# Twelve mixing matmuls in a row, and other places for the side work of an output projection

## The chip, the cores and the metric

The kernel runs on one core of a Trainium2 chip. The metric is the time of one execution on the device in microseconds; lower is better.

## The reference

One layer of a chunked gMLP block with a widened inner dimension, then a last RMSNorm. With DEPTH = 1 only mixer A runs. All values are float32; x is (1, 1024, 2048), the inner width E is 4096.

```python
CHUNK, A_GROUPS = 128, 8

def rmsnorm(x, g):
    y = x * lax.rsqrt(jnp.mean(x * x, axis=-1, keepdims=True) + EPS)
    return y * g

def gmlp_mixer(h, w_in, v_gain, w_s, b_s):
    z = h @ w_in                                    # (1024, 2048) @ (2048, 3 * 4096)
    u, v, gate = jnp.split(z, 3, axis=-1)
    u = gelu(u)
    v = rmsnorm(gelu(v), v_gain)
    vc = v.reshape(bsz, seq // CHUNK, CHUNK, A_GROUPS, A_GROUP_DIM)
    sv = einsum('gpq,bnqgc->bnpgc', w_s, vc) + b_s.T[None, None, :, :, None]
    return u * sv.reshape(bsz, seq, D_INNER), gate

h = rmsnorm(x, a_norm)
y, gate = gmlp_mixer(h, a_w_in, a_v_gain, a_w_s, a_b_s)
x = x + (y * silu(gate)) @ a_w_out                  # (1024, 4096) @ (4096, 2048)
out = rmsnorm(x, final_norm)
```

## The kernel before, in words

**Products.** Both projections are done by a seven-product scheme on 2 x 2 blocks (Strassen's): each operand of a product is a block or the sum or difference of two blocks (A_OF, B_OF), and a product goes into one or two blocks of the result. Each operand is split into a high and a low part (split, L84: ScalarE makes hi, VectorE makes lo), and each matmul is three (mm3, L89: hi*hi at L91, hi*lo at L92, lo*hi at L93). A step is one k-range of 256 rows: 2 x 4 x 3 = 24 matmuls of 128 x 512.

**Input projection.** 12 strips of columns: first four strips with v, then eight strips, one for each group g, with u and gate. In a strip seven products (IN_ORDER) of four steps each. Feeding runs two steps ahead (feed(i + AHEAD): w_sum and w_lo on VectorE, w_hi on ScalarE, into six "hl" slots, so three steps' pairs), loads three steps ahead (LOADS, on SP's queue).

**Mixing.** Of group g it runs beside products in two halves of four chunks each (apply_spatial): the first half in product 6 of its own strip (k = 6), the second half in product 1 of the next strip (k = 10); that of the last group in the first product of the output projection. A half uses four PSUM banks: two tiles of two banks each (bank_set), chunk m in bank m % 2 of tile m // 2. A chunk takes three matmuls (sv) and one VectorE instruction that reads them (L312, with the bias and u * silu(gate)). The two pairs of PSUM tiles alternate between the products and the mixing, so the product that starts two steps after a second half uses its banks next.

**Side work.** Results of the mixing are transposed in 32 x 32 blocks on VectorE (finish_y, four transposes an item, 16 items a half) and stored to DRAM through POOL's queue (L345); the output projection loads them back from there (load_y, L141, POOL's queue). Such items wait in a list `later` with a cost each; after the matmuls of each step `work(us)` takes items until their costs reach its argument (2.8 by default). Items in `soon` (readers of finished products) are all taken, and their costs count too.

**Output projection.** Seven products (OUT_ORDER = 3, 5, 2, 4, 1, 7, 6), each for two column halves s of eight steps. In s = 0 the a operand is fed (a_sum, a_hi, a_lo: two more VectorE operations), and s = 1 uses the same tiles; they take 16 slots of tag "ax" for a product, except steps 5 to 7 of the first product, which take "big" slots. The residual x is loaded into 16 "big" tiles o (L456), the products are added to them (L462), and their squares are summed on ScalarE (squares, L469).

**Last norm.** The gain of the norm is loaded into two "ax" tiles fn_b (L509) and multiplied in by items times_fn (L476). finish_rows(h, m) sums the squares of 128 rows (L482), takes the root (L81 on VectorE, L82 on POOL), scales four blocks (L490 on VectorE, L492 on ScalarE) and stores them (L494, SP's queue). The first half of the rows (h = 0) is finished from `later` during the last product; the second half behind the last matmuls, which are ordered row block by row block (L532).

**Order.** The program is written in this order; a scheduler then places each instruction on its engine's queue by that order and by what it depends on, and puts in the waits. Each engine and each DMA queue works off its own queue in order.

Of the kernel before, what the change touches and what calls it, by code (L numbers as in the profile page):

```python
# [10 lines left out]
ALU = mybir.AluOpType  # L11
# [8 lines left out]
A_OF = {1: (11, 1, 22), 2: (21, 1, 22), 3: (11,), 4: (22,), 5: (11, 1, 12), 6: (21, -1, 11), 7: (12, -1, 22)}  # L20
B_OF = {1: (11, 1, 22), 2: (11,), 3: (12, -1, 22), 4: (21, -1, 11), 5: (22,), 6: (11, 1, 12), 7: (21, 1, 22)}
IN_ORDER = (1, 2, 5, 4, 3, 7, 6)
OUT_ORDER = (3, 5, 2, 4, 1, 7, 6)
# [7 lines left out]
def gmlp_kernel(ctx, tc, x, xT, g_in, w_in, gain, wsT, bsT, w_out, fnorm, out):  # L31
    nc = tc.nc
# [3 lines left out]
    HCH = NCH // 2  # L36
    HT = S // 2
    G = wsT.shape[0]
    C = E // G
    CB = C // P  # L40
    JI = D // P // 4
    JO = E // P // 4
# [9 lines left out]
    def slot(tag, name, dt=F32):  # L52
        return main.tile([P, 2, C], dt, tag=tag, name=name, bufs=SLOTS[tag])

    def bank_set(n, name):

        return [ps.tile([P, 2, 512], F32, tag=f"set{n}_{t}", name=f"{name}_{t}") for t in range(2)]
# [20 lines left out]
    def inv_rms(ss, width, r):  # L78

        m = m_all if ss.shape[1] > 1 else main.tile([P, 1], F32, tag="m_inv", name="m_inv", bufs=2)  # L80
        nc.vector.tensor_scalar(out=m, in0=ss, scalar1=1.0 / width, scalar2=EPS, op0=ALU.mult, op1=ALU.add)  # L81
        nc.gpsimd.tensor_tensor(out=r, in0=m, in1=mhalf[:, : ss.shape[1]], op=ALU.pow)  # L82
# [6 lines left out]
    def mm3(acc, ah, al, bh, bl, start, stop, on=False):  # L89

        nc.tensor.matmul(out=acc, lhsT=ah, rhs=bh, start=start, stop=False, skip_group_check=on)  # L91
        nc.tensor.matmul(out=acc, lhsT=ah, rhs=bl, start=False, stop=False, skip_group_check=on)  # L92
        nc.tensor.matmul(out=acc, lhsT=al, rhs=bh, start=False, stop=stop, skip_group_check=on)  # L93

    def combine(of, load, tag, name):

        if len(of) == 1:
            return load(of[0])
        a, b = load(of[0]), load(of[2])
        s = slot("sum", name)  # L100
        nc.vector.tensor_tensor(out=s, in0=a, in1=b, op=ALU.add if of[1] > 0 else ALU.subtract)  # L101
        return s
# [4 lines left out]
    outs = [(0, C), (2 * C, 3 * C)]  # L107
# [83 lines left out]
    def feed(i):  # L191

        if i >= len(steps):
            return
        kind, s, p, j = step = steps[i]
        first = kind == "in" and s == 0
        if first or (kind == "out" and s == 0):
            load = h_block if first else load_y
            raw = combine(A_OF[p], lambda b: load(step, b), "sum", "a_sum")

            tag = "big" if kind == "out" and p == OUT_ORDER[0] and j >= JO - 3 else "ax"
            parts = [slot(tag, f"a_{l}", F32R) for l in ("hi", "lo")]
            split(raw, *parts)
            aparts[i] = parts
            if first:
                for t, d in zip(parts, a_dram[p, j]):
                    nc.gpsimd.dma_start(out=d, in_=t.bitcast(F32))
        elif kind == "out":
            aparts[i] = aparts[i - JO]
        raw = combine(B_OF[p], lambda b: load_w(step, b), "sum", "w_sum")  # L210
        wparts[i] = [slot("hl", f"w_{l}", F32R) for l in ("hi", "lo")]
        split(raw, *wparts[i])


    soon, later = [], []

    def work(us=2.8):
        while soon or (later and us > 0):
            cost, what = (soon or later).pop(0)
            us -= cost  # L220
            what()

    def work_all():
# [7 lines left out]
        out=eye, in_=ones[:, 0, :P], pattern=[[-1, P]], compare_op=ALU.is_equal, fill=0.0, base=0, channel_multiplier=1)  # L231
    ss_x, r_ps = bank_set(1, "ss_x")
    order_x = [(jj, h) for j in range(JI) for jj in (j, JI + j) for h in range(2)]
    for n, (jj, h) in enumerate(order_x):
        t = hx[jj, h] = slot("big", "x_t")
        nc.sync.dma_start(
            out=t, in_=xT[jj * 2 * P:(jj + 1) * 2 * P, h * HT:(h + 1) * HT].rearrange("(u p) c -> p u c", p=P))
# [16 lines left out]
    for h in range(2):  # L254
        for n in range(HCH):
            nc.vector.tensor_scalar(
                out=d_x[:, h, n * P:(n + 1) * P], in0=eye, scalar1=rx[:, h * HCH + n:h * HCH + n + 1], scalar2=None,
# [47 lines left out]
    def apply_spatial(g, half, n_set, prod):  # L305
        banks = bank_set(n_set, f"sv{g}_{half}")
        for m in range(HCH):
            sv = banks[m // 2][:, m % 2]
            wh, wl, vh, vl = spatial[half * HCH + m]
            mm3(sv, wh, wl, vh, vl, True, True)  # L310
            y = prod[m // 2][:, m % 2]
            nc.vector.scalar_tensor_tensor(  # L312
                out=y, in0=sv, scalar=bs_sb[:, g:g + 1], in1=y, op0=ALU.add, op1=ALU.mult)
        for m in range(HCH):
            for part in range(P // Q):
                later.append((1.2, lambda m=m, part=part: finish_y(g, half, m, part, prod[m // 2])))
# [55 lines left out]
    for s in range(len(strips)):  # L372
# [5 lines left out]
        if is_v:  # L378
            gains = slot("ax", "gain_b")
            nc.gpsimd.dma_start(  # L380
                out=gains.rearrange("p a b -> p (a b)"),
# [64 lines left out]
    fn_b = []  # L446
# [25 lines left out]
    def times_fn(s, block, t, cs=(0, 1)):  # L472
        n = outs[s][block % 10 - 1] // C
        for c in cs:
            d = acc[s, block][t][:, c]
            nc.vector.tensor_tensor(out=d, in0=d, in1=fn_b[n // 2][:, n % 2], op=ALU.mult)  # L476

    def finish_rows(h, m):

        ss = main.tile([P, 1], F32, tag="ss", name="ss", bufs=4)  # L480
        ro = main.tile([P, 1], F32, tag="ro", name="ro", bufs=4)
        nc.vector.tensor_reduce(out=ss, in_=sso[h][:, m], axis=mybir.AxisListType.X, op=ALU.add)  # L482
        inv_rms(ss, D, ro)
        r0 = (h * HCH + m) * P
        for s in range(2):
            for n in range(2):
                block = 10 * (h + 1) + n + 1
                d = acc[s, block][m // 2][:, m % 2]
                if n == 0:
                    nc.vector.tensor_scalar(out=d, in0=d, scalar1=ro, scalar2=None, op0=ALU.mult)  # L490
                else:
                    nc.scalar.activation(out=d, in_=d, func=AF.Copy, scale=ro)  # L492
                col = outs[s][n]
                nc.sync.dma_start(out=out[r0:r0 + P, col:col + C], in_=d)  # L494

    n_set = a
    for p in OUT_ORDER:
        for s in range(len(outs)):
            n_set ^= 1
            banks = bank_set(n_set, f"o{p}_{s}")  # L500
            last = p == OUT_ORDER[-1] and s == 1
            for j in range(JO):
                if j == JO // 2:
                    for block, _ in TO_C[p]:
                        init_acc(s, block)
                    if p == OUT_ORDER[-1] and s == 0:
                        for n in range(2):
                            fn_b.append(slot("ax", f"fn_b{n}"))
                            nc.gpsimd.dma_start(  # L509
                                out=fn_b[n].rearrange("p a b -> p (a b)"),  # L510
                                in_=fnorm[:, 2 * n * C:2 * (n + 1) * C].broadcast_to([P, 2 * C]))
                        for s_, block in finished:
                            for t in range(2):
                                later.append((1.4, lambda s_=s_, block=block, t=t: times_fn(s_, block, t)))
                        for m in range(HCH):
                            later.append((1.2, lambda m=m: finish_rows(0, m)))
                if p == OUT_ORDER[0] and s == 0 and j < 3:
                    spatial_step(8 + j, *before)
                advance(i)
                if not last or j < JO - 2:  # L520
                    products(i, banks, True)
                work()
                i += 1
            if last:

                work_all()
                for m in range(HCH):
                    for ii in (i - 2, i - 1):
                        products(ii, banks, True, (m,))
                    block = DONE_AFTER[p][0]  # L530
                    d = acc[s, block][m // 2][:, m % 2]
                    nc.vector.tensor_tensor(out=d, in0=d, in1=banks[m // 2][:, m % 2], op=ALU.add)  # L532
                    squares(s, block, m // 2, (m % 2,))
                    times_fn(s, block, m // 2, (m % 2,))
                    finish_rows(1, m)
                continue
            for t in range(2):
                soon.append((1.2 * len(TO_C[p]), lambda p=p, s=s, t=t, banks=banks: add_to(s, p, t, banks)))
            for block in DONE_AFTER[p]:
                finished.append((s, block))  # L540
                for t in range(2):
                    soon.append((0, lambda s=s, block=block, t=t: squares(s, block, t)))
                    if p == OUT_ORDER[-1]:
                        later.append((1.4, lambda s=s, block=block, t=t: times_fn(s, block, t)))


# [32 lines left out]
```

## Time and profile before

| | |
|---|---|
| median of 3 runs | 2641.49 us (2640.5 to 2643.14) |
| the profiled execution | 2639.87 us |
| its span in the profile | 2638.2 us |
| TensorE, matmuls | 2538.4 us busy, 96% of the span, 10980 matmuls |
| VectorE | 1801.9 us busy, 68% |
| ScalarE | 856.6 us busy, 32% |
| mean granted TensorE clock | 0.982 |
| DMA | 701.92 MB, mean 266 GB/s |

The rows of the timeline are: start, duration, engine, line, operation, output<-inputs, sizes, count; in brackets the idle time of the engine before the instruction and what released it. A name such as w_lo stands for all buffers of that name. A row of waits reads: who waited, for whom, us in total, times, longest. Matmuls overlap: one lasts 0.39 us in the rows, but the next starts 0.23 us after it.

### The profile page before, as it was taken

What the parts mean: (1) busy time and instruction counts of PE and PEld (TensorE: products, weight loads), DVE (VectorE), ACT (ScalarE), POOL (GpSimd) and SP (SyncE); (2) the same over time, 40 slices, a digit from 0 to 9 for tenths busy, and PEclk for the clock granted to TensorE, in tenths of its full rate; (3) what the DMA queues carried; (4) which work ended last, traced back from release to release, by engine and by line L of the source; (5) the groups of instructions that cost most, each with busy time, mean ns of one, the idle gap of its engine ahead of it and who ended that gap; (6) DMA issues with size and microseconds to landing.
All of it is one profiled execution on the core that took longest, in us unless ns stands there. A gap on an engine that the chain in (4) does not pass through costs nothing.

```text
span 2638.2 us, 29702 instructions
## 1 busy us (share of the span) xinstructions
PE 2538.4 (96%) x10980; PEld 2076.4 (79%) x10980; DVE 1801.9 (68%) x2466; ACT 856.6 (32%) x1008; POOL 163.7 (6%) x289
## 2 busy tenths in 40 slices
PE   6999999999999999999999999999999999999997
PEld 3887888888887887878878788787887788888876
DVE  6984545546458768587685876858769946577776
ACT  4452332323233232322423224233243223233233
POOL 1220000000000000000000000000010211011010
PEclk8999999999999999999999999999999999999999
DMA  8998786959685785856858568586695856669884
GB/s 311 352 414 310 290 294 225 362 200 362 236 303 189 238 315 190 316 196 245 316 180 314 212 239 327 173 297 239 215 355 179 302 200 222 225 228 320 288 296 167
DMA packets 250049, 701.92 MB, mean 266 GB/s; under 512 B 21665, under 2 KB 21681, under 8 KB 249905
## 3 DMA queue, kind: packets, MB, share of 16 engines
q1 hardware_dynamic: 210816, 557.91, 59.3%
q0 software_dynamic: 39088, 142.11, 14.2%
q8 instruction: 87, 1.43, 0.2%
q14 instruction: 58, 0.47, 0.1%
HBM read 628.63 MB, written 71.30 MB: 265 GB/s over the span
## 4 chain that ended last, share of the span: by engine, by line
PE 79%; DVE 11%; issue 5%; DMA 4%; POOL 0%; ACT 0%; SPq 0%; POOLq 0%; ACTq 0%; DVEq 0%
PE m L93 21%; PE m L92 20%; PE m L91 20%; PE o L93 6%; PE o L92 6%; PE o L91 6%; DVE y_t L341 4%; DVE w_lo L87 2%; DMA w_raw<-in_w_in 2%; DMA x_t<-in_xT 1%; DVE c L312 1%; DVE w_sum L101 1%; DMA y_raw<-y 1%; DVE u L418 1%; DVE o L476 1%
## 5 line engine op out<-in xcount | busy, mean ns | idle before, releaser
L92 PE MATMUL m<-w_lo,a_hi 128*128 128x512 f32 x2688 | 1050.8, 391 | 7.1 <-DVE w_lo L87 7.1
L91 PE MATMUL m<-w_hi,a_hi 128*128 128x512 f32 x2688 | 1052.1, 392 | 3.8 <-ACT a_hi L86 3.5
L93 PE MATMUL m<-w_hi,a_lo 128*128 128x512 f32 x2688 | 1052.3, 391 | 0.0
L87 DVE TENSOR_TENSOR w_lo<-w_sum,w_hi 128x1024 fp32r<-128x1024 f32 x320 | 391.2, 1223 | 387.6 <-ACT w_hi L86 386.7
L86 ACT ACTIVATE w_hi<-w_sum 128x1024 fp32r<-128x1024 f32 x320 | 339.3, 1060 | 950.7 <-PE m L92 623.2
L92 PEld LDWEIGHTS m<-w_lo,a_hi 128*128 128x128 f32 x2688 | 507.9, 189 | 115.0 <-DVE w_lo L87 8.8
L91 PEld LDWEIGHTS m<-w_hi,a_hi 128*128 128x128 f32 x2688 | 508.2, 189 | 112.7 <-ACT a_hi L86 5.0
L93 PEld LDWEIGHTS m<-w_hi,a_lo 128*128 128x128 f32 x2688 | 508.3, 189 | 106.8 <-DVE a_lo L87 0.6
L101 DVE TENSOR_TENSOR w_sum<-w_raw 128x1024 f32<-128x1024 f32 x319 | 388.3, 1223 | 113.6 <-DMA w_raw<-in_w_in 101.2
L92 PE MATMUL o<-w_lo,a_hi 128*128 128x512 f32 x896 | 350.8, 391 | 9.7 <-DVE w_lo L87 9.7
L93 PE MATMUL o<-w_hi,a_lo 128*128 128x512 f32 x896 | 349.9, 391 | 2.2 <-DVE a_lo L87 2.2
L91 PE MATMUL o<-w_hi,a_hi 128*128 128x512 f32 x896 | 350.1, 391 | 1.6 <-DVE m_inv L81 1.4
L341 DVE STREAM_TRANSPOSE y_t<-c 32x128 f32<-32x128 f32 x1024 | 309.8, 303 | 15.6
L86 ACT ACTIVATE w_hi<-w_raw 128x1024 fp32r<-128x1024 f32 x128 | 135.5, 1060 | 510.4 <-PE m L92 360.3
L87 DVE TENSOR_TENSOR w_lo<-w_raw,w_hi 128x1024 fp32r<-128x1024 f32 x128 | 156.6, 1223 | 173.5 <-ACT w_hi L86 172.9
L92 PEld LDWEIGHTS o<-w_lo,a_hi 128*128 128x128 f32 x896 | 169.0, 189 | 47.9 <-DVE w_lo L87 12.8
L91 PEld LDWEIGHTS o<-w_hi,a_hi 128*128 128x128 f32 x896 | 169.0, 189 | 37.9 <-DVE m_inv L81 1.8
L93 PEld LDWEIGHTS o<-w_hi,a_lo 128*128 128x128 f32 x896 | 168.9, 189 | 38.0 <-DVE a_lo L87 3.1
L86 ACT ACTIVATE a_hi<-a_sum 128x1024 fp32r<-128x1024 f32 (+1 forms) x61 | 63.4, 1044 | 132.2 <-DVE a_sum L101 122.4
L141 POOL DMA_DIRECT2D y_raw<-y x96 | 50.9, 531 | 495.7 <-DVE w_sum L101 206.4
L87 DVE TENSOR_TENSOR a_lo<-a_sum,a_hi 128x1024 fp32r<-128x1024 f32 (+1 forms) x61 | 73.2, 1203 | 11.3 <-ACT a_hi L86 11.3
L91 PE MATMUL sv<-v_hi,ws_hl 128*128 128x512 f32 x64 | 29.6, 463 | 47.2 <-DVE c L312 47.2
(88 smaller groups left out, 1119.0 us busy)
## 6 DMA issues: line engine op xcount, KB each, us to landing
w_raw<-in_w_in SPq DMA_DIRECT2D x224, 512.0 KB, 6.8
w_raw<-in_w_out SPq DMA_DIRECT2D x192, 512.0 KB, 6.7
y_raw<-y POOLq DMA_DIRECT2D x96, 512.0 KB, 6.6
a_hi<-a_0h SPq DMA_DIRECT2D x77, 512.0 KB, 5.3
a_lo<-a_0l SPq DMA_DIRECT2D x77, 512.0 KB, 5.2
a_hi<-a_1h SPq DMA_DIRECT2D x77, 512.0 KB, 6.0
a_lo<-a_1l SPq DMA_DIRECT2D x77, 512.0 KB, 4.9
a_hi<-a_2h SPq DMA_DIRECT2D x77, 512.0 KB, 5.8
```

Of the source, the lines that this page charges most:

```text
L86: nc.scalar.activation(out=hi, in_=raw, func=AF.Copy)
L87: nc.vector.tensor_tensor(out=lo, in0=raw, in1=hi.bitcast(F32), op=ALU.subtract)
L91: nc.tensor.matmul(out=acc, lhsT=ah, rhs=bh, start=start, stop=False, skip_group_check=on)
L92: nc.tensor.matmul(out=acc, lhsT=ah, rhs=bl, start=False, stop=False, skip_group_check=on)
L93: nc.tensor.matmul(out=acc, lhsT=al, rhs=bh, start=False, stop=stop, skip_group_check=on)
L101: nc.vector.tensor_tensor(out=s, in0=a, in1=b, op=ALU.add if of[1] > 0 else ALU.subtract)
L141: nc.gpsimd.dma_start(out=yraw[key], in_=y_dram[g][block // 10 - 1][:, b:b + 2, :])
L312: nc.vector.scalar_tensor_tensor(out=y, in0=sv, scalar=bs_sb[:, g:g + 1], in1=y, op0=ALU.add, op1=ALU.mult)
L341: nc.vector.transpose(out=yt[q * Q:(q + 1) * Q, :, c * P + i * Q:c * P + (i + 1) * Q], in_=yv[i * Q:(i + 1) * Q, :, q, :])
L418: nc.vector.tensor_tensor(out=cs[block][t], in0=cs[22][t], in1=banks[t], op=ALU.add)
L476: nc.vector.tensor_tensor(out=d, in0=d, in1=fn_b[n // 2][:, n % 2], op=ALU.mult)
```

## The change

In apply_spatial the loop over the four chunks is split in two: first all twelve matmuls, then the four readers. The rest touches the output projection: which slots some a operands take, how much side work a step takes, when fn_b is loaded, when the first half of the rows is finished, which engine scales which block, and, in the last rows, a tile of its own for the product with the gain.

```diff
@@ feed
-            tag = "big" if kind == "out" and p == OUT_ORDER[0] and j >= JO - 3 else "ax"
+            out_j = j if kind == "out" else -1
+            tag = "big" if (p == OUT_ORDER[0] and out_j >= JO - 4) or (p == OUT_ORDER[-1] and out_j == JO - 1) else "ax"
@@ apply_spatial
             wh, wl, vh, vl = spatial[half * HCH + m]
             mm3(sv, wh, wl, vh, vl, True, True)
+        for m in range(HCH):
+            sv = banks[m // 2][:, m % 2]
             y = prod[m // 2][:, m % 2]
             nc.vector.scalar_tensor_tensor(
                 out=y, in0=sv, scalar=bs_sb[:, g:g + 1], in1=y, op0=ALU.add, op1=ALU.mult)
@@ finish_rows
-    def finish_rows(h, m):
+    ros, last_block = {}, {}
+
+    def scale_rows(h, m):
         ss = main.tile([P, 1], F32, tag="ss", name="ss", bufs=4)
         ro = main.tile([P, 1], F32, tag="ro", name="ro", bufs=4)
         nc.vector.tensor_reduce(out=ss, in_=sso[h][:, m], axis=mybir.AxisListType.X, op=ALU.add)
         inv_rms(ss, D, ro)
+        ros[h, m] = ro
+
+    def finish_rows(h, m):
+        ro = ros.pop((h, m))
         r0 = (h * HCH + m) * P
         for s in range(2):
             for n in range(2):
                 block = 10 * (h + 1) + n + 1
                 d = acc[s, block][m // 2][:, m % 2]
-                if n == 0:
+                if (s, block) == (1, 22):
+                    d = last_block[m]
+                if n == s:
                     nc.vector.tensor_scalar(out=d, in0=d, scalar1=ro, scalar2=None, op0=ALU.mult)
                 else:
                     nc.scalar.activation(out=d, in_=d, func=AF.Copy, scale=ro)
@@ loop of the output projection
-                    if p == OUT_ORDER[-1] and s == 0:
+                    if p == OUT_ORDER[-2] and s == 1:
                         for n in range(2):
                             fn_b.append(slot("ax", f"fn_b{n}"))
...
                                 later.append((1.4, lambda s_=s_, block=block, t=t: times_fn(s_, block, t)))
+                    if p == OUT_ORDER[-1] and s == 1:
                         for m in range(HCH):
-                            later.append((1.2, lambda m=m: finish_rows(0, m)))
+                            later.append((0.3, lambda m=m: scale_rows(0, m)))
+                        for m in range(HCH):
+                            later.append((0.9, lambda m=m: finish_rows(0, m)))
...
-                work()
+                work(2.8 if s == 1 else 0.6 if len(A_OF[p]) > 1 else 1.6)
@@ last rows
                     squares(s, block, m // 2, (m % 2,))
-                    times_fn(s, block, m // 2, (m % 2,))
+                    if m % 2 == 0:
+                        scaled = slot("hl", "o_fn")
+                    n = outs[s][block % 10 - 1] // C
+                    nc.vector.tensor_tensor(out=scaled[:, m % 2], in0=d, in1=fn_b[n // 2][:, n % 2], op=ALU.mult)
+                    last_block[m] = scaled[:, m % 2]
+                    scale_rows(1, m)
                     finish_rows(1, m)
@@ behind a product
-                    if p == OUT_ORDER[-1]:
+                    if fn_b:
                         later.append((1.4, lambda s=s, block=block, t=t: times_fn(s, block, t)))
```

## The prediction

> **What bounds the kernel now.** I read the page first, then the waits of TensorE, then busy time by stretches, then the timeline of the stretches where time is lost. The page's line of engines:
>
> ```profile
> PE 2538.4 (96%) x10980; PEld 2076.4 (79%) x10980; DVE 1801.9 (68%) x2466; ACT 856.6 (32%) x1008; POOL 163.7 (6%) x289
> ```
>
> TensorE is the bound, VectorE is second. The waits of TensorE (total us, times, longest):
>
> ```profile
> PE sv L91 <- DVE c L312: 47.2, 8, 6.4
> PE o L92 <- DVE w_lo L87: 9.7, 7, 2.8
> PE o L93 <- DVE a_lo L87: 2.2, 2, 1.4
> PE o L91 <- DVE m_inv L81: 1.4, 1, 1.4
> ```
>
> The largest is the wait the diff aims at: mixing matmuls (sv) wait for the VectorE reader of other mixing results, eight times, once a half. The others belong to the output projection. Stretches (length, busy time and count of each engine, granted clock, DMA):
>
> ```profile
> core 0: us, PE busy (x) PEld busy (x) DVE busy (x) ACT busy (x) POOL busy (x), PEclk, DMA share, GB/s
> 841.00:842.00 1.00, 1.00 (x4) 0.71 (x4) 0.39 (x2) 0.00 (x0) 0.00 (x0) 0.50 0.00 0
> 846.00:848.00 2.00, 2.00 (x10) 1.64 (x9) 1.70 (x5) 0.00 (x0) 0.00 (x0) 1.00 0.00 0
> 1984.00:2030.00 46.00, 42.57 (x180) 34.38 (x179) 44.84 (x89) 16.75 (x16) 1.26 (x2) 0.96 0.48 156
> 2030.00:2100.00 70.00, 62.79 (x269) 49.54 (x268) 63.14 (x102) 17.70 (x17) 14.94 (x25) 1.00 0.76 265
> 2100.00:2500.00 400.00, 400.00 (x1767) 331.31 (x1766) 257.32 (x221) 125.73 (x149) 35.64 (x65) 1.00 0.72 249
> 2560.00:2610.00 50.00, 45.95 (x194) 37.10 (x193) 42.93 (x62) 18.14 (x26) 2.23 (x4) 0.97 0.61 209
> 2600.00:2605.00 5.00, 5.00 (x24) 4.14 (x23) 3.18 (x4) 1.06 (x1) 0.00 (x0) 1.00 0.00 0
> 2610.00:2638.00 28.00, 15.46 (x67) 11.90 (x65) 10.26 (x25) 8.23 (x16) 2.16 (x4) 0.87 0.41 150
> ```
>
> The undisturbed stretch 2100 to 2500 gives the pace: 400 us / 1767 = 0.2264 us a matmul. Time lost in a stretch is its length less its count times that: 1984 to 2100 loses 116 - 449 x 0.2264 = 14.4 us, 2560 to 2610 loses 6.1, 2610 to 2638 loses 12.8 (most of it the unavoidable end).
>
> **Part 1, the mixing (L305 to L313), seven times in the input projection.** Timeline of one second half:
>
> ```profile
> 832.42 0.39 PE L91 MATMUL sv<-v_hi,ws_hl 128*128 128x512 f32 x1
> 832.62 6.64 DVE L341 STREAM_TRANSPOSE y_t<-c 32x128 f32<-32x128 f32 x21
> 839.30 0.75 DVE L312 SCALAR_TENSOR_TENSOR c<-sv,bs_sb,c 128x512 f32<-128x512 f32 x1
> 840.10 0.79 PE L91 MATMUL sv<-v_hi,ws_hl 128*128 128x512 f32 x1 [6.38 <-DVE c L312]
> 1007.22 0.79 PE L91 MATMUL sv<-v_hi,ws_hl 128*128 128x512 f32 x1 [6.38 <-DVE c L312]
> ```
>
> Two groups of three run (the second starts at 832.42); a third starts only when the reader L312 of 839.30 is done. That reader reads another bank of the same two-bank PSUM tile, so the wait goes by whole tiles. On VectorE it stands behind 21 transposes (6.64 us, 0.316 each). From the clock column: after this idle stretch TensorE runs at 0.50 at 841 and is at 1.00 only by 846. The price of one stall comes from the period: 1007.22 - 840.10 = 167.12 us for 28 steps of 24 matmuls and 24 mixing ones, 696 x 0.2264 = 157.6, lost 9.5 us: some 6.5 of idling and 3 of half clock.
>
> The edit puts all twelve matmuls ahead of the four readers in program order. No matmul then depends on a reader of its own half. The cost: the reader of m=0 now waits for the group of m=1, same tile, at least one group of 3 x 0.23 = 0.7 us later; hidden, as VectorE is busy with the 21 transposes until 839.3 anyway. Nothing is added to or taken from any engine. So 7 x 9.5 = 66.5 us would go, if nothing else is late.
>
> What is late next is VectorE. Today the stall lets it catch up:
>
> ```profile
> 841.79 1.41 DVE L312 SCALAR_TENSOR_TENSOR c<-sv,bs_sb,c 128x512 f32<-128x512 f32 x2 [0.61 <-PE sv L93]
> 846.23 0.75 DVE L312 SCALAR_TENSOR_TENSOR c<-sv,bs_sb,c 128x512 f32<-128x512 f32 x1 [1.44 <-PE sv L93]
> 850.28 1.23 DVE L87 TENSOR_TENSOR w_lo<-w_raw,w_hi 128x1024 fp32r<-128x1024 f32 x1 [1.06 <-ACT w_hi L86]
> 855.72 1.23 DVE L87 TENSOR_TENSOR w_lo<-w_raw,w_hi 128x1024 fp32r<-128x1024 f32 x1 [4.00 <-ACT w_hi L86]
> 879.78 1.23 DVE L87 TENSOR_TENSOR w_lo<-w_raw,w_hi 128x1024 fp32r<-128x1024 f32 x1
> 876.39 1.06 ACT L86 ACTIVATE w_hi<-w_raw 128x1024 fp32r<-128x1024 f32 x1 [4.38 <-PE m L92]
> 881.83 1.06 ACT L86 ACTIVATE w_hi<-w_raw 128x1024 fp32r<-128x1024 f32 x1 [4.38 <-PE m L92]
> ```
>
> ScalarE starts a w_hi whenever TensorE ends a step and frees its buffer, so its rows mark the steps: 881.83 - 876.39 = 5.44 us. VectorE idles 0.61 + 1.44 + 1.06 + 4.00 = 7.1 us between 839 and 856 and is nearly always busy from there to 881. The w_lo that ends at 879.78 + 1.23 = 881.0 is needed by the second matmul of the step of 881.83, at 882.05: a margin of 1.05 us. With the stall gone TensorE comes 9.5 us earlier and VectorE, if its order stays, 7.1: 1.05 - 9.5 + 7.1 = -1.35. TensorE then waits about 1.3 us for w_lo, once a strip. Ends: 0 (transposes placed elsewhere) and 3.5 (a run of a dozen transposes, 3.8 us, put ahead of that w_lo). I take 1.3, the value of the rows themselves. The four readers end before the next user of their banks, two steps later: 834.5 + 2 x 5.44 = 845.4 against 839.3 + 3.0 = 842.3. **Sum of part 1: -66.5 + 7 x 1.3 = -57.**
>
> A rule of the Trainium skill bears on the size of what remains: page "TensorE: Matmul & The Clock Gate", section "Part 1: The HAM clock gate (the 'warmup' mystery)", says that the clock falls to half after an idle window of about 3.4 us and returns after a busy one. The trace agrees at both sides, by 6.38 above and 2.60 below. By that rule 1.3 us costs no clock, and the sum stays as it is.
>
> **Part 2, the eighth half and the side work of the first product (work(2.8) to 1.6 or 0.6).**
>
> ```profile
> 2008.37 0.51 PE L91 MATMUL sv<-v_hi,ws_hl 128*128 128x512 f32 x1 [2.60 <-DVE c L312]
> 2008.71 0.40 PE L92 MATMUL sv<-v_lo,ws_hl 128*128 128x512 f32 x1
> 2037.95 1.23 DVE L87 TENSOR_TENSOR w_lo<-w_sum,w_hi 128x1024 fp32r<-128x1024 f32 x1
> 2044.30 1.23 DVE L87 TENSOR_TENSOR w_lo<-w_sum,w_hi 128x1024 fp32r<-128x1024 f32 x1
> 2084.11 1.23 DVE L101 TENSOR_TENSOR a_sum<-y_raw 128x1024 f32<-128x1024 f32 x1 [2.46 <-DMA y_raw<-y]
> 2092.77 1.23 DVE L101 TENSOR_TENSOR a_sum<-y_raw 128x1024 f32<-128x1024 f32 x1 [2.73 <-DMA y_raw<-y]
> ```
>
> The eighth stall is 2.60 us and the clock does not fall (0.40 a matmul right behind). Here VectorE is the local bound: one w_lo every 6.35 us against a 5.44 us step, and 44.84 + 63.14 = 108 of 116 us busy. Three side items a step are 12 transposes, 3.8 us; with 1.6 it is two, 2.5. In steps of s=0 that is 1.3 us less, but the 32 items have to be done and end two or three steps later, in s=1. So VectorE's work up to 2096 is the same; only its 8 idle us can be won, 5.2 of them waits for y_raw loads. These loads stand on POOL's queue behind stores of transposed y, which now go later. The tag change moves the two operand tiles of step 4 from "ax" (16 slots) to "big" (25); a missing big slot delays one load, at most a step. Ends: -14.4 (all lost time goes) and +5.4 (a late y_raw costs one step). I take -5, nearest to the 5.2 us that VectorE waits for the loads.
>
> **Part 3, fn_b eight steps earlier, finish of the first half eight steps later.**
>
> ```profile
> 2556.68 2.50 DVE L476 TENSOR_TENSOR o<-o,fn_b 128x512 f32<-128x512 f32 x4 [2.90 <-DMA fn_b<-in_fnorm]
> 2572.61 0.55 PE L92 MATMUL o<-w_lo,a_hi 128*128 128x512 f32 x1 [2.67 <-DVE w_lo L87]
> 2583.88 0.50 PE L93 MATMUL o<-w_hi,a_lo 128*128 128x512 f32 x1 [1.39 <-DVE a_lo L87]
> 2582.72 11.16 SPq L494 DMA_DIRECT2D out<-o  x16
> ```
>
> Today the products with the last norm's gain start at 2556.68, fall into a half whose steps already need four VectorE operations of 1.2 us, and TensorE waits 2.67 and 1.39 us; with the clock this is the 6.1 us of 2560 to 2610. After, ten of the items (1.25 us each) start in the product before, two a step beside w_sum and w_lo (2.4 + 2.5 = 4.9 of 5.44 us), and at most one a step goes into the last s=0, where a step then needs 4.8 + 1.25 = 6.05: four such steps and two feeding steps of 7.3 add about 8 us of lag to a lead of two steps, 10.9 less the 2.3 of making a w_lo. Cover is thin, so 1 us is left: -5; ends -6.1 and 0. The a operands of the last step move from ax to big, since fn_b holds two of the 16 ax slots; big has 16 output tiles, these two, and 7 for loads of two a step: nothing. fn_b's two loads go on POOL's queue ahead of the y_raw loads of the last product; the wait for them (2.90 today) only fills idle time of VectorE. The 16 stores of the first half go from 2582 to about 2606; SP issues them in 11.16 us, the DMA is empty there (share 0.00 at 2600 to 2605), and they end before the last rows' stores from 2620 on: nothing; without that room, up to 3 us.
>
> **Part 4, the last rows.**
>
> ```profile
> DVE o L476 <- ACT sq_o L469: 2.5, 3, 0.8
> 2618.39 0.69 DVE L476 TENSOR_TENSOR o<-o,fn_b 128x512 f32<-128x512 f32 x1 [0.85 <-ACT sq_o L469]
> 2623.82 0.50 PE L91 MATMUL o<-w_hi,a_hi 128*128 128x512 f32 x1 [1.38 <-DVE m_inv L81]
> ```
>
> The product goes to a tile of its own, so it no longer waits for the squares (three waits, 2.5 us), and VectorE gets to the add that holds the last matmuls back (1.38) sooner. On the last row's own chain only the product of 0.69 goes. Ends -0.7 and -4; I take -2.5, the waits. Exchanging which block ScalarE scales moves nothing: two and two before and after.
>
> **Sum.** -57 - 5 - 5 - 2.5 = -69.5: span 2638.2 to 2568.7, and the profiled execution's 2639.87 to 2570.4. The median of the runs lies 1.6 above that execution: 2572 us.
>
> **Rivals.** (a) VectorE keeps up everywhere and the out phase gains more: all 66.5, -10, -6 and -3: 2556. For it: VectorE is busy for only 68% of the span. Against it: the margin of 1.05 us. (b) The wait moves: VectorE becomes the bound after each half and about 4.5 us of waiting for w_lo return (more transposes ahead of it, as today's runs of 22). Gain per strip 9.5 - 4.5 = 5.0, or 2.0 if the half clock's 3 us come back too; 2641.5 - 35 - 12.5 = 2594, or 2615. The skill's rule of 3.4 us would give the second, no row here tells which, since none lies between 2.60 and 6.38. (c) The change doesn't do what it says: the mixing matmuls still run in pairs with a wait, because something else holds the second tile: only parts 2 to 4, 2629. Against: TensorE's first two groups already write both tiles without waiting. (d) Slower: the readers, now one after another, get ordered behind two runs of 22 transposes (2 x 7 us); the last reader ends at 856 instead of 842, and the next user of the banks, due at 845.4, waits 11 us with 3 of half clock: 14 instead of 9.5, seven times, 2641.5 + 32 - 12.5 = 2661. It decides from 11.3 us a strip on (9.5 and a seventh of the 12.5).
>
> **How the numbers follow.** Forecast 0.64, (a) 0.17, (b) 0.11, (c) 0.05, (d) 0.03. The forecast's own range is 2560 to 2585 by the ends of parts 1 to 4. The range for 8 in 10 takes in (a) and the near end of (b): 2554 to 2594. A measurement of this kernel can tell about 0.2%, 5 us, from no change. Faster: all but (d) and a mishap of the size of (c): 0.96; same 0.01; slower 0.03.
>
> **What would show it.** Right: no wait of sv on L312; twelve sv matmuls 0.23 us apart; clock 1.00 through the strips; a period of 158 to 160 us between second halves; at most a short wait on w_lo some seven steps behind a second half; products with fn_b before 2480; no 0.85 us waits in the last rows. Wrong: a wait of a strip's matmuls on w_lo or on L312 above 3 us, clock 0.50 anywhere between 800 and 2000, or waits for y_raw or w_raw of a step's length in the output projection.

## The result, and the profile after

The changed kernel takes 2576.72 us (median of 4 executions, 2574.9 to 2577.48) against 2641.78 of the kernel before in the same comparison: a ratio of 0.9753, 95% interval 0.9736 to 0.977. The prediction said 2572, range 2554 to 2594. The profiled execution took 2576.23 us, its span is 2574.2; before, the span was 2638.2. So 64.0 us of span have to be placed.

Both programs run the same 10980 matmuls in the same order of stages, so the start of the n-th matmul cuts both spans at the same work. This table is worked out from those starts (numbers 3431, 8301, 8701, 10501 and 10901); the strips are the seven that hold a second half.

| us | start | strips | first output product | middle | late products | tail | span |
|---|---|---|---|---|---|---|---|
| before | 825.9 | 1170.0 | 105.8 | 408.0 | 97.0 | 31.5 | 2638.2 |
| after | 827.6 | 1112.9 | 105.1 | 408.0 | 90.7 | 29.9 | 2574.2 |
| difference | +1.8 | -57.2 | -0.7 | 0.0 | -6.3 | -1.6 | -64.0 |
| predicted | 0 | -57 | -5 | 0 | -5 | -2.5 | -69.5 |

The start holds nothing that the diff touches; over all runs here it lies between 825.8 and 827.6, so the +1.8 is no effect of the change.

The page of the changed kernel, its line of engines, and then its waits of TensorE (who waited, for whom, total us, times, longest):

```profile
PE 2521.1 (98%) x10980; PEld 2063.7 (80%) x10980; DVE 1799.6 (70%) x2466; ACT 856.0 (33%) x1008; POOL 164.7 (6%) x289
```

```profile
PE m L92 <- DVE w_lo L87: 12.7, 11, 4.2
...
PE o L92 <- DVE w_lo L87: 8.8, 5, 4.7
...
PE o L91 <- DVE o L549: 0.8, 1, 0.8
```

The row of before with 47.2 us, mixing matmuls behind a reader of other mixing results, is gone. Of the 12.7 us of the first row, 7.1 lie ahead of the strips; from there on what is left of TensorE's waiting is nearly all for w_lo, that is for VectorE. The same view for the strips alone (800 to 1930 us):

```profile
PE m L92 <- DVE w_lo L87: 5.6, 7, 0.8
```

Seven waits, one a strip. TensorE's timeline shows the first and last of twelve mixing matmuls, that short wait, and the first mixing matmul of the next second half:

```profile
833.52 0.39 PE L91 MATMUL sv<-v_hi,ws_hl 128*128 128x512 f32 x1
...
836.01 0.39 PE L93 MATMUL sv<-v_hi,ws_hl 128*128 128x512 f32 x1
...
875.52 0.50 PE L92 MATMUL m<-w_lo,a_hi 128*128 128x512 f32 x1 [0.81 <-DVE w_lo L87]
...
992.59 0.39 PE L91 MATMUL sv<-v_hi,ws_hl 128*128 128x512 f32 x1
```

Eleven gaps between 833.52 and 836.01 are 0.226 us each: the twelve run as one block. The period is 992.59 - 833.52 = 159.07 us, where it was 167.12. VectorE in the same place:

```profile
834.13 6.97 DVE L345 STREAM_TRANSPOSE y_t<-c 32x128 f32<-32x128 f32 x22
841.14 1.23 DVE L87 TENSOR_TENSOR w_lo<-w_raw,w_hi 128x1024 fp32r<-128x1024 f32 x1
842.28 2.72 DVE L316 SCALAR_TENSOR_TENSOR c<-sv,bs_sb,c 128x512 f32<-128x512 f32 x4
...
874.24 1.22 DVE L87 TENSOR_TENSOR w_lo<-w_raw,w_hi 128x1024 fp32r<-128x1024 f32 x1
```

The queue of 22 transposes is still there, 6.97 us long. The readers still wait behind it and end at 845.0, but TensorE no longer waits for them. The w_lo of 874.24 ends at 875.46, and the matmul that needs it starts at 875.52: this is the 0.81. Stretches of the changed kernel (length, busy time and count of each engine, granted clock, DMA):

```profile
core 0: us, PE busy (x) PEld busy (x) DVE busy (x) ACT busy (x) POOL busy (x), PEclk, DMA share, GB/s
800.00:1930.00 1130.00, 1124.43 (x4947) 927.21 (x4946) 871.94 (x1477) 367.30 (x392) 41.78 (x67) 1.00 0.73 265
841.00:842.00 1.00, 1.00 (x6) 0.84 (x5) 0.97 (x2) 0.35 (x1) 0.00 (x0) 1.00 0.00 0
1960.00:2040.00 80.00, 71.07 (x292) 56.06 (x290) 72.00 (x129) 19.69 (x19) 14.21 (x24) 0.96 0.75 252
2500.00:2550.00 50.00, 50.00 (x223) 41.39 (x222) 34.38 (x46) 18.09 (x27) 3.21 (x4) 1.00 0.71 238
2550.00:2574.00 24.00, 13.06 (x56) 9.96 (x54) 10.04 (x24) 8.13 (x16) 2.16 (x4) 0.89 0.47 175
```

The microsecond 841 to 842, at clock 0.50 before, is at 1.00, and so are the strips as a whole. The late products (2500 to 2550) run without a gap. The first output product (within 1960 to 2040) still loses time: 80 - 292 x 0.2264 = 13.9 us.

### The profile page after: what moved, and what is told of

Same layout as the page of the kernel before. It is cut to its first block, busy times and chain, and to the rows that moved or that the text cites. A ratio compares the mean times of both kernels' runs of the same rounds, so it can differ in the third digit from the quotient of the medians.

```text
span 2574.2 us, 29714 instructions
## 1 busy us (share of the span) xinstructions
PE 2521.1 (98%) x10980; PEld 2063.7 (80%) x10980; DVE 1799.6 (70%) x2466; ACT 856.0 (33%) x1008; POOL 164.7 (6%) x289
## 5 line engine op out<-in xcount | busy, mean ns | idle before, releaser
L92 PE MATMUL m<-w_lo,a_hi 128*128 128x512 f32 x2688 | 1049.8, 391 | 12.7 <-DVE w_lo L87 12.7
L409 DVE TENSOR_TENSOR u<-u,m 128x1024 f32<-128x1024 f32 x48 | 58.3, 1219 | 14.7 <-PE m L93 13.4
```

What stands on the lines that cost most here:

```text
L409: soon.append((1.2, lambda t=t: nc.vector.tensor_tensor(out=cs[22][t], in0=cs[22][t], in1=banks[t], op=ALU.subtract)))
```

## The experiments

Ratios are to the kernel before.

**One part alone, and all but that part.**

```diff
 e1_row_only: before, with this alone          e2_all_but_row: after, without it
             mm3(sv, wh, wl, vh, vl, True, True)
+        for m in range(HCH):
+            sv = banks[m // 2][:, m % 2]
             y = prod[m // 2][:, m % 2]
```

> The kernel before with part 1 alone: the twelve mixing matmuls ahead of the four readers. Theory (the wait goes by whole two-bank PSUM tiles and stands behind the transposes): all of the gain in the strips is here, 57 us between the first second half and the output projection, and the eighth stall; the output projection keeps its waits on w_lo and a_lo (about 6 us at the late product with the gain): 2641.8 - 57 - 2 = 2583. Rival (the strips gain because less side work stands in VectorE's queue): under 15 us, above 2627.

Measured: 2583.65 us, 0.9786 (0.9771 to 0.98).

> The changed kernel with part 1 undone. Theory: the strips keep the period of 167.1 us and the eight stalls on the reader; only the output projection gains, 6 us at the last norm and 1.6 in the last rows: 2641.8 - 8 = 2634. Rival (the parts need each other): 2641 or more, or a period in the strips below 165.

Measured: 2632.61 us, 0.997 (0.9959 to 0.998). The waits of TensorE in the first and in the second:

```profile
PE m L92 <- DVE w_lo L87: 12.8, 11, 3.9
PE o L92 <- DVE w_lo L87: 12.7, 9, 3.3
...
PE o L93 <- DVE a_lo L87: 1.6, 1, 1.6
PE o L91 <- DVE m_inv L81: 1.4, 1, 1.4
```

```profile
PE sv L91 <- DVE c L314: 47.3, 8, 6.4
```

The strips take 1113.0 and 1167.5 us, the late products 97.6 and 90.7. So the split loop alone carries the 57 us, and the rest of the diff alone carries the late 6.3 and the tail's 1.6. The two parts do not need each other: each stage is as long as in whichever kernel has its edit. (The strips are 2.5 us shorter in the second run than before, though the stalls in them are as long, 44.7 and 44.6 us in all. By the clock records TensorE worked 35.5 us of the strips at half clock in the second run and 41.0 before; half of the difference is lost time, 2.8 us. The last section shows why equal stalls cost unequal time.)

**What the wait hangs on: program order, or the two-bank tile?**

```diff
 e3_pairs: after, with the loops nested
-        for m in range(HCH):        # all twelve matmuls, then the four readers
+        for t in range(2):
+            for m in (2 * t, 2 * t + 1):   mm3(...)
+            for m in (2 * t, 2 * t + 1):   nc.vector.scalar_tensor_tensor(...)
```

> The changed kernel with the mixing in two pairs: matmuls of chunks 0 and 1 (one PSUM tile), their two readers, matmuls of chunks 2 and 3 (the other tile), their two readers. Theory (the wait is between a reader and a later matmul of the same two-bank tile): no wait, as fast as the changed kernel, 2576.7 within 2 us, no row in which sv waits for a reader. Rival (any reader placed ahead of a matmul in the program holds it up, tile or not): the third group waits for the readers as before, about 2640.

Measured: 2577.01 us, 0.9762 (0.9747 to 0.9776), strips 1112.9, and no wait of sv. The first two readers stand ahead of the last six matmuls in program order and hold nothing up, as they read the other tile. The dependence goes by whole two-bank tiles, not by program order as such.

**The same stall, met from the other side.** If the price was the queue of transposes ahead of the reader, taking the queue away must do without the split.

```diff
 e4_no_transposes_ahead: before, input projection
-                work()
+                work(0 if (s >= NV and p == 6 and j >= 2) or (s > NV and p == 1 and j < 2) else 2.8)
```

> The kernel before, with no side items taken in the four steps ahead of a second half (last two of product 6, first two of product 1), so that no transposes stand ahead of the first reader. Theory (the length of the stall is VectorE's queue of transposes): the wait of sv shrinks from 6.4 to 1.5 us or less, the granted clock stays at 1.00, and the period falls from 167.1 to 159 to 161 us, as 36 transposes (11 us) now come later and make TensorE wait for w_lo by some us: about 2595. Rival (the wait is a cost of the dependence itself, whatever stands in the queue): 6 us of wait stay, 2640.

Measured: 2593.23 us, 0.982 (0.9804 to 0.9837), strips 1121.2. The waits of TensorE for a reader in the whole run, and all its waits in the strips (800 to 1930 us):

```profile
PE sv L91 <- DVE c L312: 0.6, 1, 0.6
```

```profile
PE m L92 <- DVE w_lo L87: 8.4, 21, 0.6
```

With the old order of matmuls and readers the stall of 6.38 us is gone from all seven strips (the 0.6 lies in the output projection). So its length was the run of transposes. The side work that is pushed away returns as 21 short waits on w_lo: VectorE's work is the same, and its free time lies elsewhere.

**The residual wait of 0.8 us.**

```diff
 e7_two_items: after, input projection
-                work()
+                work(2.8 if is_v else 2.4)
```

> The changed kernel with two side items a step instead of three in the strips with mixing. Theory (the wait of 0.8 us on w_lo seven steps behind a second half is VectorE's queue of transposes): the seven waits go and the period falls from 159.07 to 158.0 us: 2576.7 - 6.5 = 2570. Rival (the same transposes end later and collide with the two VectorE readers of the next products): a wait on w_lo appears later in the strip, 2576 or more.

Measured: 2575.04 us, 0.9751 (0.9737 to 0.9766), not to be told from the changed kernel. The seven waits stay, 4.5 us in all instead of 5.6, and move a step later: two items a step instead of three spread the same VectorE work, they do not lessen it.

**Why the first output product gained nothing.** Four edits ask whether it is the budget of side work, the slots of step 4, or the loads of the residual o:

```diff
 e5_side_28: after, the old budget in the first output product
-                work(2.8 if s == 1 else 0.6 if len(A_OF[p]) > 1 else 1.6)
+                work(2.8 if s == 1 or p == OUT_ORDER[0] else 0.6 if len(A_OF[p]) > 1 else 1.6)
 e6_tag3: after, the old slots
-            tag = "big" if (p == OUT_ORDER[0] and out_j >= JO - 4) or ...
+            tag = "big" if (p == OUT_ORDER[0] and out_j >= JO - 3) or ...
 e8_late_o: after, the loads of o four steps later
-                if j == JO // 2:
+                if j == (JO - 1 if p == OUT_ORDER[0] and s == 1 else JO // 2):
 e9_o_behind: after, the loads of o of the first product's s = 1 behind its last step
-                if j == JO // 2:
+                if j == JO // 2 and not (p == OUT_ORDER[0] and s == 1):
...
+            for block, _ in TO_C[p]:          # behind the last step of a product
+                init_acc(s, block)
```

> The changed kernel with three side items a step again in s=0 of the first product of the output projection. Theory A (fewer items a step delay the last stores of transposed y, and the y loads of the second product stand behind them on POOL's queue): the wait of 4.67 us with its half clock falls to 2.8 or less, and the loss of 6.3 us late in the first product shrinks, but the waits early in it return: 2576 within 3 us. Theory B (VectorE's work up to there is the same, only its place moves): the same total with waits elsewhere. Rival C (the deferral gains): 2580 or more.

> The changed kernel with the operands of step 4 of the first product in ax again, as before the change (two more big slots free). Theory (the y loads of the second product wait for big slots): the wait of 4.67 us for y shrinks, since two more big slots are free from step 4 on: some 4 us faster, 2573. Rival (the room in ax is needed by the operands beside the mixing): a wait on a_lo or a_hi returns in the first product, 2577 to 2585.

> The changed kernel with the residual loads of s=1 of the first product issued at step 7 instead of 4, so that four big slots stay free for the y loads of the second product. Theory (y loads wait for big slots): the wait of 4.67 us for y goes and with it the half clock, 5 to 6 us faster, 2571. Rival (the loads wait for POOL's queue behind the last stores of y): nothing gained there, and the add of the first product waits for the late residual: 2577 or more.

> The changed kernel with the residual loads of s=1 of the first product of the output projection put behind that product in the program, so that the y loads of the second product get their big slots first. Theory S (the time lost late in the first product, 6.3 us, is y loads that wait for big slots): the wait of 4.67 us on w_lo goes, 5 us faster, 2571. Theory V (VectorE's work up to there sets the time): the same within 1.5 us, 2576.

Measured: 2576.64 (0.9757, 0.9742 to 0.9772), 2576.76 (0.9756, 0.974 to 0.9772), 2576.36 (0.9755, 0.9741 to 0.977) and 2575.68 (0.9757, 0.9743 to 0.9772); first product 107.0, 105.8, 106.6 and 105.1 us. None moves it by more than 2 us. (The last two did move loads: those of o went from 2003.68 and 2012.31 on, in place of 1980.21, and three y_raw loads of the second product at 1987, in place of 2001.70 to 2007.92. So slots for these loads are not what holds the product up. The y_raw loads behind the last store of y stayed at 2019 and later.)

Two edits on the amount of VectorE's work, one by leaving work out and one by moving it to GpSimd:

```diff
 e10_fewer_transposes: after, finish_y
+        if g == G - 1 and half == 1:
+            if i == 0:
+                nc.vector.tensor_copy(out=yt[:, :, c*P:(c+1)*P], in_=y[:, c]...)
+        else:
             for q in range(P // Q):
                 nc.vector.transpose(...)
 e11_sum_on_pool: e7_two_items, first output product
-        nc.vector.tensor_tensor(out=s, in0=a, in1=b, ...)        # w_sum
+        nc.gpsimd.tensor_tensor(out=s, in0=a, in1=b, ...)
```

> The changed kernel with the transposes of the last group's second half left out: each chunk's 16 are replaced by one copy, so the output is another one. It takes about 4 x (16 x 0.31 - 0.6) = 17 us of VectorE's work out of the first product of the output projection. Theory V (VectorE's work sets the time there): nearly all that TensorE loses between 1960 and 2040 (71 of 80 us busy, with the half clock some 12 us) goes, 2566 or less. Theory S (big slots for the y loads): the early waits go and the late one stays, 2572 or more.

> The kernel with two side items a step in the strips, and w_sum of the first product of the output projection made by GpSimd instead of VectorE (16 operations of 1.2 us less for VectorE). Theory V: VectorE's load a step falls from 6.2 to 5.0 us, below the step of 5.44, and the loss there shrinks by 6 us or more, 2569. Rival (GpSimd makes a sum too slowly, or its DMA issues wait behind the sums): TensorE waits for w_hi and w_lo instead, 2575 to 2590.

Measured: 2560.81 us (0.9701, 0.9685 to 0.9717) with the first product at 91.6 us, 13.5 less than after; and 2573.63 us (0.975, 0.9735 to 0.9764) with 104.1, where e7_two_items has 105.6. The stretch of the first:

```profile
1960.00:2040.00 80.00, 79.73 (x350) 65.36 (x349) 68.67 (x80) 25.75 (x25) 16.41 (x27) 1.00 0.93 332
```

58 matmuls more than after in the same 80 us, and TensorE waits for no w_lo in the whole output projection. But this edit also lets the last stores of y go earlier, and the y_raw loads behind them. The last run keeps the 64 transposes, into a tile that nobody reads, and frees only the stores from them.

```diff
 e12_transposes_aside: after, finish_y
+        aside = g == G - 1 and half == 1
+        if aside and c == 0 and i == 0:
+            for cc in range(2):
+                nc.vector.tensor_copy(out=yt[:, :, cc*P:(cc+1)*P], in_=y[:, cc]...)
         for q in range(P // Q):
             nc.vector.transpose(
-                out=yt[...],
+                out=scratch[q*Q:(q+1)*Q] if aside else yt[...],
```

> The changed kernel, but the 64 transposes of the last group's second half go to a scratch tile that nobody reads, and two copies (0.42 us each) a pair of chunks, at its first item, fill the stored tile instead (left out: these chunks are stored untransposed). VectorE's work stays the same and in the same place, 1.7 us more; only the two last stores of y no longer wait for the transposes. Theory V, that the amount of VectorE's work sets the first product of the output projection: 105 to 107 us, total 2576 to 2578.5. Rival C, that the chain does (last transposes, store of y behind them on GpSimd's queue, the y_raw loads behind the store, then a sum on VectorE that holds up the w_lo behind it): the store goes some 10 us earlier, the wait of 4.6 us for y_raw and that of 4.7 us for w_lo shrink or go, the first product takes 92 to 100 us, total 2563 to 2571.

Measured: 2578.47 us, 0.9766 (0.9752 to 0.9779), first product 105.1 (the stages between it and the late products take 1.5 us more). GpSimd's queue, the last store of y, first after the change and then in this run:

```profile
2019.35 0.73 POOL L349 DMA_DIRECT2D y<-y_t  x1 [4.56 <-DVE y_t L345]
```

```profile
2005.85 0.72 POOL L354 DMA_DIRECT2D y<-y_t  x1 [1.57 <-DVE scratch L350]
```

The store goes 13.5 us earlier and the product is not shorter. But the y_raw loads behind the store do not go earlier, first after the change and then in this run:

```profile
2020.61 1.66 POOL L141 DMA_DIRECT2D y_raw<-y  x3 [0.53 <-DVE w_sum L101]
```

```profile
2022.46 1.67 POOL L141 DMA_DIRECT2D y_raw<-y  x3 [5.87 <-DVE w_sum L101]
```

They now wait for a sum of VectorE. So this run clears the store alone as a cause, not the loads. TensorE waits in the same places; the longest after the change, and those of this run around it:

```profile
2033.06 0.79 PE L92 MATMUL o<-w_lo,a_hi 128*128 128x512 f32 x1 [4.67 <-DVE w_lo L87]
```

```profile
2016.95 0.50 PE L92 MATMUL o<-w_lo,a_hi 128*128 128x512 f32 x1 [1.80 <-DVE w_lo L87]
2024.49 0.50 PE L92 MATMUL o<-w_lo,a_hi 128*128 128x512 f32 x1 [1.80 <-DVE w_lo L87]
2032.89 0.63 PE L92 MATMUL o<-w_lo,a_hi 128*128 128x512 f32 x1 [2.65 <-DVE w_lo L87]
```

One long wait became several short ones. The runs e10 and e12 differ in the 64 transposes on VectorE, and by 13.5 us: VectorE's work sets the time of this product. VectorE is busy for 97.9 of its 105.1 us after the change, and for 82.2 of 91.6 in e10. Whether the work acts directly, ahead of each w_lo in VectorE's queue, or also through the loads, which wait for VectorE's sums, is not parted: in e10 the stores and loads went earlier too. Waits for loads do not set it by themselves, as VectorE waits longer for y_raw in e10 than after the change (6.5 us), and TensorE waits for no w_lo there (1960 to 2045):

```profile
DVE a_sum L101 <- DMA y_raw<-y: 8.1, 4, 3.3
```

Why the move of the sums to GpSimd gained only 1.5 us shows in its waits of GpSimd (1960 to 2045), a GpSimd row and a VectorE row:

```profile
POOL w_sum L101 <- DVE w_lo L87: 26.7, 7, 6.4
```

```profile
1999.78 2.40 POOL L101 TENSOR_TENSOR w_sum<-w_raw 128x1024 f32<-128x1024 f32 x1 [3.74 <-DVE w_lo L87]
...
2011.96 2.41 POOL L101 TENSOR_TENSOR w_sum<-w_raw 128x1024 f32<-128x1024 f32 x1
```

```profile
2011.68 3.78 DVE L87 TENSOR_TENSOR w_lo<-w_sum,w_hi 128x1024 fp32r<-128x1024 f32 x1 [2.85 <-ACT w_hi L86]
```

Seven times GpSimd starts a sum only when VectorE has made the w_lo before, so the sums did not run ahead but lengthened the way from one w_lo to the next, by 2.40 us where VectorE needs 1.22. And beside such a sum a w_lo took 3.78 us in place of 1.23. That this chain is all of the missing gain is argued from these rows, not tested.

## Why the prediction was right or wrong, point by point

**Part 1: right.** Predicted -57, measured -57.2, and e1 puts it on the split loop alone. The mechanism holds step by step: by whole tiles (e3), priced by the run of transposes (e4), with the half clock gone (841 to 842 at 1.00). The forecast residual, one short wait on w_lo some seven steps behind a second half, is there in each strip: 0.8 us for 1.3. The period of 159.07 lies in the 158 to 160 named, 1.5 above the 157.6 without loss. The prediction's "once a half" counts second halves alone: the first halves had no such wait. By the rule of the Trainium skill that the prediction names, a wait of 1.3 us would cost no clock; the measured 0.81 did not (the next matmuls start 0.23 to 0.34 us apart). But the prediction misread its own trace on that rule. It saw agreement "at both sides" in a wait of 2.60 us without half clock, and no wait between 2.60 and 6.38. The clock did fall behind the 2.60, 1.35 us after the wait's end, as the last section shows, and the same trace has waits of 2.67, 2.76 and 3.85 us. Rival (a), in which VectorE keeps up everywhere, falls with the seven waits that are left, and (b), (c) and (d) with the same rows: no wait of 4.5 us, no wait of sv, and readers that end at 845.0 with no one waiting for them.

**Part 2: the term that was mis-sized.** Predicted -5, measured -0.7. The failing step is the choice "nearest to the 5.2 us that VectorE waits for the loads". That VectorE's work up to 2096 stays the same, and that the stores ahead of the loads go later, was rightly said in the same place; but VectorE's waits for y_raw were taken as time that can be won. They grow, from 5.2 us in this product to 6.5. VectorE's waits after the change, 1960 to 2045:

```profile
DVE a_sum L101 <- DMA y_raw<-y: 6.5, 3, 4.6
```

And e12 shows that an earlier store wins nothing, as the loads behind it then wait for VectorE. The price was VectorE's work itself, which the diff moves and does not lessen: e10, with 64 transposes of 0.303 us less and four copies of 0.42 more, 17.7 us, gains 13.5. One sign of being wrong that the prediction named came true here: the clock is at 0.50 before 2000, from 1991.66 on, behind a wait of 1.78 us for w_lo.

**Part 3: right, slightly more than forecast.** Predicted -5 with -6.1 as the end, measured -6.3. The reserved 1 us for thin cover was not needed: TensorE waits for nothing from 2500 to 2550. The cover was thicker than the prediction's sum said: its steps add 4 x 0.61 + 2 x 1.86 = 6.2 us of lag, not 8. VectorE's timeline shows the products with the gain where they were forecast, before 2480:

```profile
2445.62 3.70 DVE L480 TENSOR_TENSOR o<-o,fn_b 128x512 f32<-128x512 f32 x6 [4.75 <-DMA fn_b<-in_fnorm]
```

The wait for fn_b is longer than before (4.75 for 2.90) and, as said, fills VectorE's idle time only. e1, which keeps the old places, keeps the loss (97.6 us, waits of 3.3 and 1.6).

**Part 4: right in kind, less in size.** Predicted -2.5, measured -1.6. The waits of 0.85 are gone and the product starts with no wait (2555.20), but not all of it reaches the end:

```profile
2555.20 0.69 DVE L555 TENSOR_TENSOR o_fn<-o,fn_b 128x512 f32<-128x512 f32 x1
...
2562.89 0.16 DVE L488 TENSOR_REDUCE ss<-sso 128x1 f32<-128x4 f32 x1 [0.50 <-ACT sq_o L473]
```

```profile
2560.83 0.50 PE L91 MATMUL o<-w_hi,a_hi 128*128 128x512 f32 x1 [0.78 <-DVE o L549]
```

One wait for the squares moved to the sum of squares (0.50), and the last matmuls still wait 0.78 us for an add, where it was 1.38.

**Sum.** The gain of span was 69.5 - 64.0 = 5.5 us smaller than forecast: 4.3 in part 2, 0.9 in part 4 and 1.8 in the start that belongs to no edit, less 1.3 from part 3 and 0.2 from part 1.

## What to carry to other kernels

If several results share one tracked tile, issue all writers of the tile before its first reader, or pair them by tile: otherwise each writer waits for whatever stands ahead of the reader on its engine. Price such a stall from the period between equal places, not from the wait alone: 9.5 us here for a wait of 6.4, as the half clock comes on top. And an engine's waits inside a stretch where it is the bound are not by themselves time to be won: ask whether the edit takes work off that engine, or only moves it.

## What the runs showed of the hardware

**When the clock falls.** In each of the fourteen traces the granted clock changes only at the edges of equal pieces of 3.41 us, on one grid that runs on through the trace (worked out from the clock records; the edges fit to 4 ns). Here is the time of before cut at these edges: the eighth stall of 2.60 us, which ends at 2008.37, and what follows; then a wait of 2.76 us that ends at 2096.32.

```profile
2006.30:2009.72 3.42, 1.35 (x6) 1.10 (x7) 3.35 (x7) 1.06 (x1) 0.72 (x1) 1.00 0.61 211
2009.72:2013.13 3.41, 3.41 (x10) 2.64 (x9) 3.35 (x8) 2.01 (x2) 0.00 (x0) 0.50 0.69 181
2091.63:2095.04 3.41, 1.93 (x9) 1.27 (x7) 2.27 (x2) 1.46 (x3) 1.02 (x3) 1.00 1.03 396
2095.04:2098.45 3.41, 2.13 (x9) 1.76 (x10) 3.41 (x4) 0.99 (x2) 1.23 (x2) 1.00 1.06 333
2098.45:2101.87 3.42, 3.42 (x17) 2.82 (x16) 3.42 (x4) 1.06 (x1) 0.55 (x1) 1.00 0.95 338
```

And of the changed kernel, with a wait of 1.78 us:

```profile
1988.25:1991.66 3.41, 1.63 (x8) 1.02 (x7) 3.37 (x7) 2.11 (x2) 0.72 (x1) 1.00 1.00 370
1991.66:1995.07 3.41, 3.41 (x10) 2.62 (x9) 3.35 (x6) 0.00 (x0) 0.00 (x0) 0.50 0.98 341
```

A piece in which TensorE idles for 2.07 us is followed by a piece at 0.50, and so is one with 1.78. The longer wait of 2.76 us is shared out over two pieces, 1.48 and 1.28 us, and costs no clock. In all traces, from 100 us on, the 58 pieces at full clock with 2.01 us of idling or more were all followed by half clock, 6 of 16 between 1.77 and 1.94 us, and none with less (idle time by the rows, in which the ends of matmuls are modelled). So it is not the length of a wait that counts, but how much of one piece is idle; where the edges lie differs from run to run. The page "TensorE: Matmul & The Clock Gate" of the Trainium skill, in the section named in the prediction, gives a window of 3413 ns that runs freely, and the rows agree; it puts the half clock behind at least one idle window, and here 2.01 us of idling in a window were always enough, so the measurement decides.

**VectorE beside GpSimd.** The w_lo of 3.78 us shown above ends at 2015.46, 1.09 us after the end of the GpSimd sum beside it (2014.37). In the same run an a_lo that starts inside a sum does the same:

```profile
1966.22 2.39 POOL L101 TENSOR_TENSOR w_sum<-w_raw 128x1024 f32<-128x1024 f32 x1 [2.81 <-DVE w_lo L87]
```

```profile
1967.12 2.57 DVE L87 TENSOR_TENSOR a_lo<-y_raw,a_hi 128x1024 fp32r<-128x1024 f32 x1
```

It ends at 1969.69, 1.08 us after the sum (1968.61); without a sum beside it such an operation takes 1.22. The other way round, a sum that starts 0.16 us into a w_lo took 3.30 us (2007.77). Transposes, which have one input, keep their time: five take 1.56 us beside the sum of 1961.01. The Trainium skill, page "SBUF — State Buffer", section "SBUF: two separate sides", says that the two engines share a pair of ports that the one that starts first holds to its end, when the VectorE instruction has two inputs there. The a_lo and the sum of 3.30 us agree; the w_lo of 3.78 us does so only in part, since by the rows it started 0.28 us ahead of its sum and was held up all the same.
